# The merge gates and the late projections of a decoder trunk, computed in pairs of column blocks with seven block products in place of eight

## The chip, the cores and the metric

One NeuronCore of a Trainium2 chip runs the kernel. The metric is the device time of one execution in microseconds (us). Before the change it is 2110.89 us, the median of three runs (2110.68 to 2111.18). Engines are called as the profile calls them: PE (TensorE, matmuls), PEld (its weight loads), DVE (VectorE), ACT (ScalarE), POOL (GpSimd) and SP (SyncE, which issues the DMAs).

## The reference, cut

A two-layer decoder trunk on 1024 tokens of width 1024, float32. Each layer runs three token mixers on one normalised input and merges them through gates:

```
h = rms_norm(x, g_pre)
p = h @ w_in                      # 1024 -> 7936 columns
u_a, v_a, gate_a, q_b, k_b, v_b, gate_b, q_c, k_c, v_c, gate_c, merge_logits = split(p)
y_a = chunk_gmlp(u_a, v_a, ...) * silu(gate_a)            # branch A
y_b = sliding_window_attention(rope(q_b), rope(k_b), v_b, sinks) * silu(gate_b)
y_c = stick_breaking_attention(q_c, k_c, v_c) * silu(gate_c)
gates = sigmoid(merge_logits + b_merge)                   # 3 x 1024 columns
merged = gates[0]*(y_a @ w_a) + gates[1]*(y_b @ w_b) + gates[2]*(y_c @ w_c)
x = x + rms_norm(merged @ w_out, g_post)
```

## The kernel before, in words

**Arithmetic.** Every operand of a large matmul is held as two fp32r tiles, a rounded part (hi) and the rest (lo), made by `split` (L101): ACT casts (L104), DVE subtracts (L105). `mm3` (L119 to 123) adds hi x hi, hi x lo and lo x hi into one PSUM bank. So one 128x128 by 128x512 block product is three matmuls of 512 columns, each with its own weight load.

**Layout.** `h`, the normalised input, lies transposed in SBUF for the whole layer: two halves of 512 tokens, each as hi and lo, eight K blocks of 128 in each. One column block of a projection is 128 columns of `w_in`: 2 halves x 8 K blocks x 3 = 48 matmuls of 512 columns. Other data live in 27 slots of 128x1024 (`new`, `done`), reused in the order in which they are given back. PSUM has two banks each under the tags `pj` and `ta` (`ptr`, `pav`), and two tiles of two banks under `z` (`pz`).

**Order.** PE's order is that of the code, fixed by hand. A scheduler orders the other engines. `queue_layer` (L234 to 353) puts projection jobs into a stream, and the branches call `fill(us)` to run so much of that stream between their own steps; `need(label)` runs it until a job is through. All loads and stores are issued by SP in one order.

**Stages of one layer.** Branch C (stick-breaking attention), then branch B (L454 to 572: 8 steps of scores, softmax, two transpositions with POOL selects at L509 and L511, and `attend`, L527), then branch A (L574 to 623, its matmuls at L611 and evacuations at L614), with fills between all steps. Then `merges` (from L638): 24 blocks of 128 output columns, for each half of the tokens 24 gate matmuls from `h` (into `pj`), the sigmoid (L674), 12 branch matmuls (into `pz`), the product of both on DVE (L678, L681) and the sum over branches on POOL (L682). Last `project_out`. `gated` (L625 to 635) multiplies a branch output with its SiLU gate (L630, L631, L632) and splits it.

## Time and profile before

| what | value |
|---|---|
| median of three runs | 2110.89 us |
| the profiled execution, its own time | 2110.61 us |
| its span in the profile | 2108.5 us |
| busy: PE / DVE / ACT / POOL | 2087.3 / 925.2 / 717.1 / 358.6 us |
| matmuls on PE | 10601 |
| moved by DMA | 169.48 MB, mean 80 GB/s |
| layer 1: branch B, branch A, merges | 368 to 536, 536 to 568, 568 to 968 us |
| layer 2: branch B, branch A, merges | 1412 to 1579, to 1612, to 2012 us |

The span is the profiled execution from its first to its last recorded instruction; 2.1 us of its own time lie outside. Busy times are sums over the span, which hold stages of different kinds: what bounds a stage is read from windows, waits and the timeline of that stage. A matmul's recorded duration (0.40 us) is longer than the distance from one start to the next, since matmuls are pipelined.

### The profile page before, as it was taken

To read this page: it belongs to the slowest core of one execution; us is meant where nothing else is said; L and a number is where in the kernel's file an instruction comes from. 1 tells how busy PE (TensorE), PEld (TensorE's weight loads), DVE (VectorE), ACT (ScalarE), POOL (GpSimd) and SP (SyncE) were. 2 spreads that over 40 slices of the span, in tenths; PEclk is the share of its full clock that TensorE was granted. 3 is DMA by queue.
4 is the path that set the end of the run, shared out by engine and by line. 5 is a ranking of instruction groups with operands and counts; after the bars stand their busy time and mean duration, and the time that the engine had idled before them with its cause. 6 is when DMAs were issued, how large, how long until landed. Compare 5 with 4: busy or idle time off the path is not lost.

```text
span 2108.5 us, 25832 instructions
## 1 busy us (share of the span) xinstructions
PE 2087.3 (99%) x10601; PEld 1752.3 (83%) x10601; DVE 925.2 (44%) x1167; ACT 717.1 (34%) x1307; POOL 358.6 (17%) x429
## 2 busy tenths in 40 slices
PE   8999999999999999999999999999999999999998
PEld 7898888898888888888888988888988888888886
DVE  5455543576522423224545545336764233232223
ACT  5334333564322212223334334245552122222221
POOL 0121211443200011110002112105431001111100
PEclk9999999999999999999999999999999999999999
DMA  4112123232412311114321112322234223121123
GB/s 160 41 51 67 54 90 90 70 91 80 170 50 77 114 60 60 40 51 140 109 71 51 41 60 66 95 80 80 71 104 166 60 60 110 50 70 51 47 84 130
DMA packets 162134, 169.48 MB, mean 80 GB/s; under 512 B 5800, under 2 KB 137952, under 8 KB 162016
## 3 DMA queue, kind: packets, MB, share of 16 engines
q1 hardware_dynamic: 162016, 167.83, 25.1%
q8 instruction: 83, 1.36, 0.3%
q14 instruction: 35, 0.29, 0.0%
HBM read 129.01 MB, written 33.55 MB: 77 GB/s over the span
## 4 chain that ended last, share of the span: by engine, by line
PE 97%; DVE 1%; ACT 0%; POOL 0%; DMA 0%; issue 0%; SPq 0%; DVEq 0%; POOLq 0%; ACTq 0%
PE pj L122 24%; PE pj L123 24%; PE pj L121 24%; PE pz L122 5%; PE pz L121 5%; PE pz L123 5%; PE ptr L398 1%; PE pav L527 1%; PE pz L469 1%; PE pav L123 1%; PE pav L122 1%; PE pav L121 1%; PE pz L229 1%; PE ptr L502 1%; DMA s<-in_x_dram 0%; POOL s L511 0%
## 5 line engine op out<-in xcount | busy, mean ns | idle before, releaser
L121 PE MATMUL pj<-h,whi 128*128 128x512 f32 x1728 | 692.4, 401 | 0.0
L122 PE MATMUL pj<-h,whi 128*128 128x512 f32 x1728 | 683.5, 396 | 0.0
L123 PE MATMUL pj<-h,wlo 128*128 128x512 f32 x1728 | 682.6, 395 | 0.0
L123 PEld LDWEIGHTS pj<-h,wlo 128*128 128x128 f32 x1728 | 324.6, 188 | 77.8
L121 PEld LDWEIGHTS pj<-h,whi 128*128 128x128 f32 x1728 | 325.0, 188 | 70.2
L122 PEld LDWEIGHTS pj<-h,whi 128*128 128x128 f32 x1728 | 325.0, 188 | 68.2
L105 DVE TENSOR_TENSOR wlo<-wr,whi 128x1024 fp32r<-128x1024 f32 x148 | 193.4, 1308 | 276.6 <-ACT whi L104 274.3
L104 ACT CAST whi<-wr 128x1024 fp32r<-128x1024 f32 x148 | 154.9, 1050 | 356.3 <-PE pj L122 316.3
L682 POOL TENSOR_TENSOR s<-s,s 128x512 f32<-128x512 f32 x56 | 78.4, 1401 | 659.8 <-DVE s L681 645.5
L121 PE MATMUL pz<-s,whi 128*128 128x512 f32 x384 | 152.0, 396 | 0.0
L122 PE MATMUL pz<-s,whi 128*128 128x512 f32 x384 | 151.7, 395 | 0.0
L123 PE MATMUL pz<-s,wlo 128*128 128x512 f32 x384 | 151.5, 394 | 0.0
L674 ACT ACTIVATE s<-pj,vec 128x512 f32<-128x512 f32 x96 | 65.9, 686 | 240.5 <-PE pj L123 240.5
L121 PE MATMUL pj<-whi,h 128*128 128x256 f32 x512 | 147.1, 287 | 0.0
L123 PE MATMUL pj<-whi,h 128*128 128x256 f32 x512 | 144.1, 281 | 0.6 <-DVE h L105 0.6
L122 PE MATMUL pj<-wlo,h 128*128 128x256 f32 x512 | 144.1, 281 | 0.6 <-DVE wlo L105 0.6
L381 DVE TENSOR_TENSOR_SCAN s<-s,ones 128x128 f32<-128x128 f32 (+3 forms) x64 | 88.4, 1382 | 98.7 <-POOL s L376 98.5
L105 DVE TENSOR_TENSOR s<-ptr,s 128x512 fp32r<-128x512 f32 (+2 forms) x132 | 77.7, 591 | 107.0 <-ACT s L104 106.6
L104 ACT CAST s<-ptr 128x512 fp32r<-128x512 f32 (+2 forms) x132 | 66.8, 506 | 118.0 <-PE ptr L398 110.1
L681 DVE TENSOR_TENSOR s<-s,pz 128x512 f32<-128x512 f32 x64 | 44.0, 687 | 137.8 <-PE pz L123 137.8
L123 PE MATMUL pj<-h,s 128*128 128x512 f32 x256 | 101.6, 397 | 0.0
L121 PE MATMUL pj<-h,s 128*128 128x512 f32 x256 | 101.4, 396 | 0.0
(138 smaller groups left out, 2775.3 us busy)
## 6 DMA issues: line engine op xcount, KB each, us to landing
wr<-in_w_in_dram SPq DMA_DIRECT2D x124, 512.0 KB, 3.8
s<-in_x_dram SPq DMA_DIRECT2D x16, 512.0 KB, 4.9
wor<-in_w_out_dram SPq DMA_DIRECT2D x16, 512.0 KB, 3.7
s<-s SPq DMA_DIRECT2D x40, 128.0 KB, 2.3
gc<-s SPq DMA_DIRECT2D x8, 512.0 KB, 2.7
oc<-s SPq DMA_DIRECT2D x8, 512.0 KB, 3.0
gb<-s SPq DMA_DIRECT2D x8, 512.0 KB, 2.9
ga<-s SPq DMA_DIRECT2D x8, 512.0 KB, 2.7
```

What stands on the lines that cost most here:

```text
L104: nc.scalar.copy(hi, raw)
L105: nc.vector.tensor_tensor(lo, raw, hi.bitcast(F32), op=ALU.subtract)
L121: nc.tensor.matmul(acc, lh, rh, start=first, stop=False)
L122: nc.tensor.matmul(acc, lh, rl, start=False, stop=False)
L123: nc.tensor.matmul(acc, ll, rh, start=False, stop=last)
L229: nc.tensor.transpose(pt[:, k], xn[:, k * P:(k + 1) * P], ident)
L381: nc.vector.tensor_tensor_scan(t1[:, :kl][:, ::-1], t1[:, :kl][:, ::-1], ones.to_broadcast([P, kl]), 1.0, op0=ALU.mult, op1=ALU.mult)
L398: nc.tensor.transpose(pt[:, b - b0], t2[:, b * P:(b + 1) * P], ident)
L469: nc.tensor.matmul(z[:, e * 2 + j], qT[e][:, n * P:(n + 1) * P], kk[i][:, k0:k0 + 256], start=i == 0, stop=i == 1)
L674: nc.scalar.activation(sg[:, ts], a, AF.Sigmoid, bias=bmv(l, xb, dm))
L681: nc.vector.tensor_tensor(sg[:, ts], sg[:, ts], z[:, ts], op=ALU.mult)
L682: eng.tensor_tensor(acc[dm][:, ts], acc[dm][:, ts], sg[:, ts], op=ALU.add)
```

## The change

34 column blocks of `w_in` a layer (two gates of branch B, the four of branch A, the four u blocks of branch A, and all 24 merge gates) leave the stream and the merges. They are computed in one stage, `dense`, behind branch B, in 17 pairs of neighbouring blocks. A pair is a 2x2 block matrix of weights (two K halves by two column blocks) times a 2x2 block matrix of `h` (two K halves by two token halves); Winograd's form of Strassen's method takes seven block products of it and sums ahead of and behind them. `Combine` makes the four sums of `h` blocks (T1 to T4) once a layer, in part during branch B. `prep` makes the seven weight operands of a pair, `prod` is one product of 12 matmuls into a bank of its own, which `bank` takes in turn from three tags (six banks). Branch A is a generator whose steps run between the first products. The SiLU gating of all branches (`gate_task`) runs beside the pairs and stores to DRAM, as do the merge gates after their sigmoid. `merges` keeps only the 12 branch matmuls of each half and loads the gates back. The first half of `w_out` is loaded in the merges (`load_wo`). The fills of branch B are cut to the smaller stream.

```diff
-FB = (10, 1.9, 1.9, 2.5, 3.2, 3.2)
-FB_MORE = {1: 2.3, 2: 1.3}
+FB = (5, 1.5, 1.5, 2.0, 2.6, 2.6)
+FB_MORE = {1: 2.0, 2: 1.0}
...
+    def bank():
+        turn[0] += 1
+        return (pj, ptr, lambda: pz()[:, :512])[turn[0] % 3]()
...
-        hi = wp.tile([P, k, n], F32R, name="whi", tag="whi", bufs=3)
-        lo = wp.tile([P, k, n], F32R, name="wlo", tag="wlo", bufs=3)
+        hi = wp.tile([P, k, n], F32R, name="whi", tag="w", bufs=6)
+        lo = wp.tile([P, k, n], F32R, name="wlo", tag="w", bufs=6)
...
-        gate("b", 0); gate("b", 1); gate("b", 2)
         raw("kb", O_KB, 1.0, after_k)
         raw("vb", O_VB, 1.0, after_v)
-        gate("b", 3)
         for hp in range(4):
             raw(("qb", hp), O_QB + hp * P, 0.125, lambda hp=hp: after_q(hp))
-            if hp < 3:
-                gate("a", hp)
-        va(0); va(1); ua(0); ua(1); ua(2); ua(3); gate("a", 3)
+            if 1 <= hp < 3:
+                gate("b", hp - 1)
+        va(0); va(1)
...
-        need("ga0")
+        need(("qb", 0))
         fill(5)
...
             pend = (v, 1, p1, o)
+            if v >= 4:
+                S["T"].go(3)
         attend(*pend)
...
+    class Combine:
+        def go(self, spare):
+            while self.left and len(free) >= 4 + spare:
+                if next(self.left, "end") == "end":
+                    self.left = None
+        def steps(self):
+            def total(hf, k0, eng):
+                r = new()
+                eng.tensor_tensor(r.rearrange("p (k t) -> p k t", k=2), h[hf][0][:, k0:k0 + 2].bitcast(F32),
+                                  h[hf][1][:, k0:k0 + 2].bitcast(F32), op=ALU.add)
+                return r
...
+            for kp in range(2):
+                k0 = kp * 2
+                r12, r11 = total(1, k0, nc.gpsimd), total(0, k0, nc.gpsimd)
+                nc.vector.tensor_tensor(r11, r12, r11, op=ALU.subtract)
+                keep("T1", r11)
+                yield
+                r22 = total(1, k0 + 4, nc.gpsimd)
+                nc.gpsimd.tensor_tensor(r12, r22, r12, op=ALU.subtract)
+                keep("T3", r12)
...
+                nc.vector.tensor_tensor(r22, r22, r11, op=ALU.subtract)
+                keep("T2", r22)
...
+                r21 = total(0, k0 + 4, nc.gpsimd)
+                nc.vector.tensor_tensor(r21, r21, r22, op=ALU.subtract)
+                keep("T4", r21)
...
+    def dense(l, S):
+        S["T"].go(0)
...
+        def prep(p):
+            col = pairs[p][0]
+            raw = []
+            for q in range(2):
+                t = wp.tile([P, 4, 256], F32, name="wr", tag="wr", bufs=2)
+                nc.sync.dma_start(t, w_in[l, q * 512:(q + 1) * 512, col:col + 256].rearrange("(k p) c -> p k c", p=P))
+                raw.append(t)
+            a11, a21, a12, a22 = (raw[q][:, :, r * P:(r + 1) * P] for q in range(2) for r in range(2))
...
+            yield op(a11)
+            yield op(a12)
...
+            nc.gpsimd.tensor_tensor(s3, a11, a21, op=ALU.subtract)
+            nc.gpsimd.tensor_tensor(a21, a21, a22, op=ALU.add)
+            nc.gpsimd.tensor_tensor(a11, a21, a11, op=ALU.subtract)
+            yield op(a11)
...
+            nc.gpsimd.tensor_tensor(a12, a12, a11, op=ALU.subtract)
+            yield op(a12)
...
+        def prod(n, nm):
+            left(n + 5)
+            w, acc = ops[n], bank()
+            for k in range(4):
+                mm3(acc, (w[:, 0, k], w[:, 1, k]), rhs(nm, k), k == 0, k == 3)
+            return acc
...
+        for p, (col, kind, what) in enumerate(pairs):
...
+            p1 = prod(n, "B11")
+            with tc.high_priority():
+                nc.scalar.copy(c12, p1)
+            add(c11, c12, prod(n + 1, "B21"))
+            add(u2, c12, prod(n + 2, "T2"))
+            if p in then:
+                then[p]()
+            add(u3, u2, prod(n + 3, "T3"))
+            p5 = prod(n + 4, "T1")
+            add(c22, u3, p5)
+            add(u2, u2, p5)
+            add(c21, u3, prod(n + 5, "T4"))
+            add(c12, u2, prod(n + 6, "B22"))
...
+                    nc.scalar.activation(out[j], out[j], AF.Sigmoid, bias=bmv(l, "abc".index(br), dm + j))
+                    nc.sync.dma_start(S["sg"][(i * KD + dm + j) * P:(i * KD + dm + j + 1) * P, :], out[j])
+            done(*out)
+            if p >= 5 and tasks:
+                tasks.popleft()()
+                if p % 2 and tasks:
+                    tasks.popleft()()
...
-                a = pj()
-                for k in range(KD):
-                    mm3(a, (wh[:, k], wlo[:, k]), (h[hf][0][:, k], h[hf][1][:, k]), k == 0, k == KD - 1)
-                nc.scalar.activation(sg[:, ts], a, AF.Sigmoid, bias=bmv(l, xb, dm))
+                z = bank()
                 for c in range(4):
-                    mm3(z[:, ts], (bh[:, c, cs], bl[:, c, cs]), (y[c][0][:, ts], y[c][1][:, ts]), c == 0, c == 3)
+                    mm3(z, (bh[:, c, cs], bl[:, c, cs]), y[c][hf], c == 0, c == 3)
...
             branch_b(l, S)
-            S["yc"] = [gated(S, "c", c) for c in range(4)]
-            branch_a(l, S)
-            while step() is not None:
-                pass
+            dense(l, S)
             mg = merges(l, S)
```

In the rows of instruction order below, `pj`, `ptr`, `pav`, `pz` are PSUM tiles, `h_72` to `h_75` are the four tiles of `h` (first half hi, lo, second half hi, lo), `s_...` are slots, `wr`, `whi`, `wlo` and `wop` are weights (raw, hi, lo, and the seven operands). PE, the end of branch B in layer 1. Before, from the transposes of the last step's first half to the job matmuls behind the last attend:

```order
L502 MATMUL ptr<-ident,s_4560 128x128 x4
L121 MATMUL pj<-h_74,whi 128x512
...
L527 MATMUL pav<-s_4770,s_2932 128x256 x2
L527 MATMUL pav<-s_4771,s_2931 128x256 x2
L527 MATMUL pav<-s_4770,s_2932 128x256 x2
L527 MATMUL pav<-s_4771,s_2932 128x256 x2
L121 MATMUL pj<-h_74,whi 128x512
...
L527 MATMUL pav<-s_4797,s_2932 128x256 x2
L527 MATMUL pav<-s_4798,s_2932 128x256 x2
L527 MATMUL pav<-s_4797,s_2932 128x256 x2
L527 MATMUL pav<-s_4798,s_2932 128x256 x2
L121 MATMUL pj<-h_72,whi 128x512
```

After, from the end of the stream's last job to the first product of `dense`:

```order
L130 MATMUL pj<-whi,h_75 128x256
L500 MATMUL ptr<-ident,s_4000 128x128 x8
L525 MATMUL pav<-s_4292,s_2657 128x256 x4
...
L500 MATMUL ptr<-ident,s_4209 128x128 x8
...
L525 MATMUL pav<-s_4352,s_2658 128x256 x2
L525 MATMUL pav<-s_4364,s_2658 128x256 x2
...
L525 MATMUL pav<-s_4365,s_2658 128x256 x2
L128 MATMUL ptr<-h_72,wop 128x512
L129 MATMUL ptr<-h_73,wop 128x512
```

The gate and projection matmuls of 512 columns that stood between the last transposes, the attends (L527 before, L525 after) and branch A are gone; transposes and attends follow each other, and the first product (`wop`) stands right behind the last attend. From the last scores (not shown) to that product PE has 21 projection matmuls of 256 columns, 38 attend matmuls and 16 transposes.

POOL at the same place. Before, the last selects and the first products of branch A:

```order
L509 AFFINE_SELECT s_4798<-s_4797 128x512
L511 AFFINE_SELECT s_4797<-s_4797 128x512
L509 AFFINE_SELECT s_4798<-s_4797 128x512
L511 AFFINE_SELECT s_4797<-s_4797 128x512
L617 TENSOR_TENSOR s_4550<-s_4550,s_5037 128x512 x2
```

After, from the sums ahead of the selects of step 6 to the first of the last sums for `Combine` (L648 is `total`, L663 the subtraction for T3, L507 and L509 are the selects, L723 to L733 the sums of weights in `prep`):

```order
L648 TENSOR_TENSOR s_4434<-h_72,h_73 128x1024
L648 TENSOR_TENSOR s_4325<-h_74,h_75 128x1024
L663 TENSOR_TENSOR s_3991<-s_4325,s_3991 128x1024
L507 AFFINE_SELECT s_4293<-s_4292 128x512
...
L723 TENSOR_TENSOR s_4451<-wr 128x512
L509 AFFINE_SELECT s_4305<-s_4305 128x512
L507 AFFINE_SELECT s_4306<-s_4305 128x512
L725 TENSOR_TENSOR wr<-wr 128x4x128
...
L648 TENSOR_TENSOR s_4406<-h_72,h_73 128x1024
L509 AFFINE_SELECT s_4364<-s_4364 128x512
...
L509 AFFINE_SELECT s_4364<-s_4364 128x512
L648 TENSOR_TENSOR s_4413<-h_74,h_75 128x1024
```

Sums of whole tiles of `h` and sums of weights now stand among the selects and ahead of the last ones. From the first of these rows to the last select there are 24 instructions: 16 selects, 4 sums of 128x1024 and 4 of 128x512. The last two totals and the last T3 stand behind them.

DVE in one pair of the new stage (L766 is the sum behind a product, L112 the subtraction of `split`, L682 and L684 the two products of `gate_task`):

```order
L766 TENSOR_TENSOR s_5834<-s_5834,ptr 128x512
L112 TENSOR_TENSOR wop<-wr,wop 128x512
L766 TENSOR_TENSOR s_5833<-s_5834,pz 128x512
L112 TENSOR_TENSOR wop<-wr,wop 128x512
L766 TENSOR_TENSOR s_5833<-s_5833,pj 128x512
L112 TENSOR_TENSOR wop<-wr,wop 128x512
L682 TENSOR_TENSOR s_5977<-s_5977,s_5978 128x1024
L766 TENSOR_TENSOR s_5835<-s_5833,ptr 128x512
L766 TENSOR_TENSOR s_5833<-s_5833,ptr 128x512
L112 TENSOR_TENSOR wop<-s_5909,wop 128x512
L684 TENSOR_TENSOR s_5977<-s_5977,s_5978 128x1024
L766 TENSOR_TENSOR s_5835<-s_5833,pz 128x512
```

Before, in the merges of the same layer (L678 the product of gate and branch, L105 the subtraction of `split`):

```order
L678 TENSOR_TENSOR s_5241<-s_5239,pz 128x512
L105 TENSOR_TENSOR wlo<-wr,whi 128x1024
L678 TENSOR_TENSOR s_5241<-s_5239,pz 128x512
L105 TENSOR_TENSOR wlo<-wr,whi 128x1024
L678 TENSOR_TENSOR s_5328<-s_5326,pz 128x512
```

Where DVE had one product per half block and one split of a whole weight tile per block, it now has a split of 128x512 and a sum for nearly every product, with the gating products between them.

## Rows read from the trace of the kernel before

**Rows 1.** The page: busy time of PE and its instructions, and the chain that ended last by engine.

```profile
PE 2087.3 (99%) x10601; PEld 1752.3 (83%) x10601; DVE 925.2 (44%) x1167; ACT 717.1 (34%) x1307; POOL 358.6 (17%) x429
...
PE 97%; DVE 1%; ACT 0%; POOL 0%; DMA 0%; issue 0%; SPq 0%; DVEq 0%; POOLq 0%; ACTq 0%
```

**Rows 2.** All waits of PE over 1 us in the whole span: line that waited, what released it, us in total, times, longest.

```profile
PE pz L229 <- DVE s L220: 9.3, 2, 8.4
PE pav L611 <- DVE s L614: 2.1, 2, 1.0
PE pav L527 <- POOL s L511: 1.8, 2, 0.9
```

**Rows 3.** Windows of layer 1: second half of branch B, branch A, merges. Columns: stretch and length, busy time of PE, PEld, DVE, ACT, POOL with instructions, granted clock, DMA share, GB/s.

```profile
460.00:545.00 85.00, 84.69 (x536) 75.69 (x535) 59.05 (x97) 45.96 (x110) 25.77 (x34) 1.00 0.33 106
545.00:568.00 23.00, 21.96 (x129) 18.88 (x128) 12.03 (x14) 4.11 (x5) 8.76 (x8) 1.00 0.39 129
568.00:968.00 400.00, 400.00 (x1716) 321.94 (x1715) 125.50 (x127) 96.35 (x117) 40.58 (x30) 1.00 0.23 73
```

**Rows 4.** PE's timeline in the merges (first two rows) and in branch B: start, duration, instruction. The 24 matmuls of one gate stand between the first two.

```profile
700.09 0.40 PE L121 MATMUL pj<-h,whi 128*128 128x512 f32 x1
...
705.69 0.39 PE L121 MATMUL pz<-s,whi 128*128 128x512 f32 x1
...
441.65 2.06 PE L469 MATMUL pz<-s,s 128*128 128x256 f32 x16
443.55 0.28 PE L121 MATMUL pj<-whi,h 128*128 128x256 f32 x1
...
448.70 0.60 PE L502 MATMUL ptr<-ident,s 128*128 128x128 f32 x4
449.06 0.36 PE L121 MATMUL pj<-whi,h 128*128 128x256 f32 x1
```

**Rows 5.** Groups of equal instructions over the whole span: line, engine, operation, shapes, count, busy time and mean ns of one, idle time before them and what ended it.

```profile
L105 DVE TENSOR_TENSOR wlo<-wr,whi 128x1024 fp32r<-128x1024 f32 x148 | 193.4, 1308 | 276.6 <-ACT whi L104 274.3
...
L682 POOL TENSOR_TENSOR s<-s,s 128x512 f32<-128x512 f32 x56 | 78.4, 1401 | 659.8 <-DVE s L681 645.5 <-issue 14.3
...
L511 POOL TENSOR_SCALAR_AFFINE_SELECT s<-s 128x512 fp32r<-128x512 f32 x64 | 58.6, 919 | 19.2 <-DVE s L105 11.4 <-issue 3.6 <-POOL s L509 1.9
L105 DVE TENSOR_TENSOR s<-ptr,s 128x512 fp32r<-128x512 f32 x84 | 57.6, 688 | 55.7 <-ACT s L104 55.4
...
L509 POOL TENSOR_SCALAR_AFFINE_SELECT s<-s 128x512 fp32r<-128x512 f32 x64 | 49.9, 782 | 117.8 <-ACT s L104 117.6
...
L681 DVE TENSOR_TENSOR s<-s,pz 128x512 f32<-128x512 f32 x64 | 44.0, 687 | 137.8 <-PE pz L123 137.8
...
L630 DVE TENSOR_TENSOR s<-s,s 128x1024 f32<-128x1024 f32 x24 | 29.8, 1246 | 64.7 <-DMA s<-gb 19.4 <-DMA s<-oa 19.2 <-DMA s<-ga 19.1
...
L282 POOL TENSOR_TENSOR s<-s,s 128x1024 f32<-128x1024 f32 x10 | 25.5, 2545 | 137.1 <-DMA s<-s 107.5 <-PE pj L123 29.6
L104 ACT CAST s<-s 128x1024 fp32r<-128x1024 f32 x24 | 25.2, 1051 | 20.5 <-DVE s L632 17.7 <-POOL s L682 2.7
...
L283 POOL TENSOR_TENSOR s<-s,s 128x1024 f32<-128x1024 f32 x10 | 24.0, 2403 | 0.0
...
L617 POOL TENSOR_TENSOR s<-s,s 128x512 f32<-128x512 f32 x16 | 20.1, 1286 | 51.3 <-DVE s L614 51.3
L104 ACT CAST s<-s 128x512 fp32r<-128x512 f32 x32 | 19.9, 620 | 95.4 <-POOL s L682 88.1 <-DVE s L682 7.3
```

**Rows 6.** A load of weights, from the page's list of DMA issues (KB each, median us to landing), and the window of the highest traffic, at the start (columns as in rows 3).

```profile
wr<-in_w_in_dram SPq DMA_DIRECT2D x124, 512.0 KB, 3.8
...
12.80:15.00 2.20, 2.20 (x11) 1.92 (x10) 1.94 (x2) 2.20 (x5) 0.00 (x0) 1.00 1.02 408
```

**Rows 7.** Timeline near the end of branch B in layer 1, DVE and POOL.

```profile
511.63 0.64 POOL L509 TENSOR_SCALAR_AFFINE_SELECT s<-s 128x512 fp32r<-128x512 f32 x1
...
512.63 1.50 DVE L494 TENSOR_TENSOR s<-s,ls 128x1024 f32<-128x1024 f32 x1
...
513.00 1.62 POOL L509 TENSOR_SCALAR_AFFINE_SELECT s<-s 128x512 fp32r<-128x512 f32 x1
...
514.05 1.65 DVE L105 TENSOR_TENSOR wlo<-wr,whi 128x1024 fp32r<-128x1024 f32 x1
...
514.69 1.50 POOL L511 TENSOR_SCALAR_AFFINE_SELECT s<-s 128x512 fp32r<-128x512 f32 x1
```

**Rows 8.** Timeline of the first rope of the queries in layer 1: ACT empties the bank, SP issues four transfers, POOL and DVE follow.

```profile
351.34 0.59 ACT L268 ACTIVATE s<-pj 128x512 f32<-128x512 f32 x1
...
351.95 2.42 SPq L281 DMA_DIRECT2D s<-s  x4
...
356.29 2.39 POOL L282 TENSOR_TENSOR s<-s,s 128x1024 f32<-128x1024 f32 x1 [29.59 <-PE pj L123]
...
364.81 2.47 DVE L326 TENSOR_TENSOR s<-s,s 64x1024 fp32r<-64x1024 f32 x2
```

**Rows 9.** The last window of the span (columns as in rows 3) and PE's first projection matmuls.

```profile
2106.00:2108.50 2.50, 0.00 (x0) 0.00 (x0) 0.00 (x0) 0.00 (x0) 0.00 (x0) 0.64 0.35 146
...
17.24 0.41 PE L121 MATMUL pj<-whi,h 128*128 128x256 f32 x1
17.45 0.41 PE L122 MATMUL pj<-wlo,h 128*128 128x256 f32 x1
```

More of the change, by code (lines that the diff above doesn't have):

```diff
@@ L602, in branch_a @@
         done(ws)
+        yield
         for g in range(4):
-            need(f"ua{g}")
-            fill(3)
             u, t = S["ua", g], new()
             for hf in range(2):
-                av = (ptr() if hf else pav()).rearrange("p (n t) -> p n t", n=4)
+                av = bank().rearrange("p (n t) -> p n t", n=4)
                 for j in range(4):
@@ new lines, in load_y @@
+    def load_y(S, br, first=False, c=None):
+        y = []
+        if first:
+            S["two"] = [[new(F32R) for _ in range(2)] for _ in range(2)]
+            two = [[t.rearrange("p (c t) -> p c t", c=2) for t in q] for q in S["two"]]
+        for c in range(4) if c is None else [c]:
+            r = new()
+            nc.sync.dma_start(r, S["y" + br][c * P:(c + 1) * P, :])
+            if first:
+                o = [(h[1][0][:, c], h[1][1][:, c]), (two[0][c // 2][:, c % 2], two[1][c // 2][:, c % 2])]
+                for hf in range(2):
+                    split(*o[hf], r[:, hf * HT:(hf + 1) * HT])
+            else:
+                if br == "a":
+                    hi, lo = (t[:, 2 * c:2 * c + 2] for t in h[1])
+                    split(hi, lo, r.rearrange("p (a t) -> p a t", a=2))
+                    o = [(hi[:, hf], lo[:, hf]) for hf in range(2)]
+                else:
+                    hi, lo = new(F32R), new(F32R)
+                    split(hi, lo, r)
+                    S["yslots"].extend((hi, lo))
+                    o = [(hi[:, hf * HT:(hf + 1) * HT], lo[:, hf * HT:(hf + 1) * HT]) for hf in range(2)]
+            done(r)
+            y.append(o)
+        return y
@@ L648, in load, with load_sg @@
                 bi, br, dm = blocks[i]
-                xb = "abc".index(br)
-                wi = load_w(w_in[l, :, O_M + xb * D + dm * P:O_M + xb * D + (dm + 1) * P], KD, P)
-                wl[i] = [wi, load_w(wbs[br][l, :, dm * P:(dm + 2) * P], 4, 256) if dm % 2 == 0 else wl[i - 1][1]]
+                wl[i] = load_w(wbs[br][l, :, dm * P:(dm + 2) * P], 4, 256) if dm % 2 == 0 else wl[i - 1]
+        def load_sg(i):
+            if i < len(blocks) and i not in sgs:
+                bi, br, dm = blocks[i]
+                sgs[i] = new()
+                nc.sync.dma_start(sgs[i], S["sg"][(bi * KD + dm) * P:(bi * KD + dm + 1) * P, :])
         load(0)
-        ys = {"c": S["yc"]}
+        load_sg(0)
+        load_sg(1)
+        ys = {"c": S["first"]}
+        S["yslots"] = []
         for i, (bi, br, dm) in enumerate(blocks):
-            (wh, wlo), (bh, bl) = wl.pop(i) if dm % 2 else wl[i]
+            bh, bl = wl.pop(i) if dm % 2 else wl[i]
             y = ys[br]
-            xb = "abc".index(br)
-            if dm == 0 and bi:
-                for c in range(len(y), 4):
-                    y.append(gated(S, br, c))
-            load(i + 1)
+            for j in (1, 2, 3):
+                load(i + j)
+                load_sg(i + j) if j < 3 else None
+            sg = sgs.pop(i)
             cs = slice((dm % 2) * P, (dm % 2 + 1) * P)
-            sg, z = new(), pz()
             if bi == 0:
@@ L688, in merges @@
                 mg.append((hi, lo))
-            elif dm >= KD - 4:
-                nb = order[bi + 1]
-                if len(free) >= 5:
-                    ys.setdefault(nb, []).append(gated(S, nb, len(ys.get(nb, []))))
-            if dm == KD - 1:
-                for t in y:
-                    done(*t)
+            if bi == 0 and dm < 4:
+                ys.setdefault("b", []).extend(load_y(S, "b", c=dm))
+            if bi == 0 and dm == KD - 1:
+                for t in S["two"]:
+                    done(*t)
+            if bi == 1 and dm < 4:
+                ys.setdefault("a", []).extend(load_y(S, "a", c=dm))
+                load_wo(l, 0, dm * 2)
+            if bi == 1 and dm == KD - 1:
+                done(*S["yslots"])
         return mg
@@ L707, in project_out @@
             nc.sync.dma_start(gpre, g_pre[l + 1].partition_broadcast(P))
-        for q in range(2):
-            for k in range(0, KD, 2):
-                raw = wp.tile([P, 2, 512], F32, name="wor", tag="wr", bufs=2)
-                nc.sync.dma_start(raw, w_out[l, k * P:(k + 2) * P, q * 512:(q + 1) * 512]
-                                  .rearrange("(k p) c -> p k c", p=P))
-                split(h[q][0][:, k:k + 2], h[q][1][:, k:k + 2], raw)
+        for k in range(0, KD, 2):
+            load_wo(l, 1, k)
         o0 = [new() for _ in range(4)]
@@ L813, in trunk @@
     for l in range(L):
-        states.append({nm: dr.tile([512, T], F32, name=f"{nm}{l}") for nm in ("ga", "gb", "gc", "oa", "ob", "oc")})
+        states.append({nm: dr.tile([512, T], F32, name=f"{nm}{l}") for nm in ("ga", "gb", "gc", "oa", "ob", "oc",
+                                                                                "ya", "yb", "yc")})
+        states[l]["sg"] = dr.tile([3 * D, T], F32, name=f"sg{l}")
     nc.scalar.preload_act_table_set("sqrt_and_others")
```

116 lines of the change are left out of this document (95 added, 21 removed).

## The prediction, made before the changed kernel ran

> **What bounds the kernel now.** I read the page's busy line and its chain first: TensorE (PE) is busy 2087.3 of 2108.5 us and holds 97% of the chain that ended last [rows 1]. The waits of PE say how little is lost to others: 9.3 us at the norm (L229), 2.1 us in branch A (L611), 1.8 us in branch B's attends (L527), over two layers [rows 2]. The windows of layer 1 agree stage by stage: 84.69 of 85 us busy in the second half of branch B, 21.96 of 23 in branch A, 400.00 of 400 in the merges, where VectorE (DVE) works 125 us and ScalarE (ACT) 96 [rows 3]. So a matmul taken away is worth its pitch, and a stall put in costs its length, as long as PE stays the bound.
>
> **The pitch.** PE's timeline in the merges starts the first of 24 matmuls of 512 columns at 700.09 and the next group at 705.69: 5.60 / 24 = 0.2333 us each. 16 score matmuls of 256 columns take 441.65 to 443.55, and with what follows them at 0.117 us each; four transposes take 0.36 us [rows 4]. The Trainium skill, page "TensorE: Matmul & The Clock Gate", section "Back-to-back issue gap", gives N/2.4 + 2.5 ns as the gap of one matmul at full clock, 215.8 ns for 512 columns, and about 131 ns in a sustained stream. By these the saving below would be estimated at 88.0 or 53.4 us; the trace shows neither, 233.3 ns, and the sum goes by that.
>
> **What goes.** 34 column blocks a layer took 2 halves x 8 x 3 = 48 matmuls each, 1632. Now 17 pairs take 7 products of 4 x 3 = 12 matmuls, 84 each, 1428. The difference is 204 a layer, 408 in all, x 0.2333 = **95.2 us** of PE. The branch products of the merges keep their number.
>
> **What PE needs from others in a pair.** One pair is 84 x 0.2333 = 19.6 us. By the group rows [rows 5] DVE has 7 splits and 7 adds of 0.69 and, for one and a half branch gates, three products of 1.25: 13.4 us. ACT has 7 casts and a copy of 0.62 (5.0) and some 3.5 activations of a whole tile at 1.05 (3.7): 8.7. GpSimd (POOL) has four 128x512 sums of 1.40: 5.6. Traffic is two 512 KB weight loads, two gate stores and, for one and a half branch gates, at most 2.25 MB, 4.25 MB in 19.6 us = 217 GB/s, where the start of the kernel moved 408, and a weight load lands in 3.8 us [rows 6]. Weight operands are made five products (14 us) ahead and six PSUM banks rotate (the diff). I cost the pair loop at nothing: the cover is PE's own 19.6 us; gone, it costs whatever a pair takes beyond them, 34 times. Merge blocks shrink to 24 x 0.2333 = 5.6 us each with at most 4.7 us of DVE (1.31/2 + 2 x 0.69 + 2 x 1.31) and 2.8 of POOL; also nothing.
>
> **What comes: the tail of branch B.** Before, gate jobs stood between its last transposes and attends. The new order of PE shows none: from the last scores on there are 21 projection matmuls of 256 columns (2.45 us), 38 attend matmuls (4.4) and 16 transposes (1.44), 8.3 us of own work, and then the first product. Meanwhile POOL's new order has, between the sums that wait for the last scores' slots and the last select, 24 instructions: 16 selects at a mean of 0.85 (0.78 and 0.92), 4 sums of 128x1024 at 2.47 and 4 of 128x512 at 1.40 [rows 5]: 13.6 + 9.9 + 5.6 = 29.1 us. The last attend (0.93) follows. PE's stall is 29.1 + 0.9 - 8.3 = **21.7 us a layer**. Lower bound: selects at 0.63 as POOL does them alone [rows 7], sums at 2.40 and 1.29, 24.9 in place of 29.1, so 17.5. Upper bound: rows 7 show a DVE two-input operation at 512.63 taking 1.50 with POOL's select beside it at 1.62, and 1.65 beside 1.50 at 514.05, in place of 0.64 for a select alone: one waits for the other. If all 8.1 us of such DVE work in this stretch stood in POOL's way on top of the 24.9, the stall would be 25.6. I take the means, since they already mix both conditions. The Trainium skill, page "SBUF — State Buffer", section "Who interferes with whom", states that a DVE operation with two SBUF inputs and a GpSimd operation that reads SBUF hold one port pair in turn, for the whole instruction. The trace agrees in rows 7; by that rule the stall would be the upper bound.
>
> **The third product waits for its operand.** It needs T2 of the second half, whose sums POOL makes only behind the last select: 2 x 2.45, DVE 1.31, POOL 2.45, ACT 1.05, and three DVE operations of 1.31, 13.6 us in series [rows 5]. PE covers 0.9 of last attend, two products and 7 matmuls (31 x 0.2333 = 7.2): **5.5 us** wait. With POOL's and DVE's fastest rows it is 5.0; with three weight splits of 0.69 put ahead on DVE it is 7.6.
>
> **Three smaller ones a layer.** Branch B now starts behind the first rope and not behind later jobs: from 351.34, when ACT empties the bank, four transfers of 2.42, POOL 2.39 + 2.40 and DVE up to 367.28 took 16 us [rows 8]; the projections of the next block and the first fill cover most, so 1.0 (0 to 2). In mid-branch the sums for T1 stand on POOL (2 x 2.45) and hold DVE's subtraction ahead of the attends' adds: 2.0 (0 to 4). After a gap the clock can be low: the granted clock is 0.64 in the last stretch, where PE has been idle, and in the first matmuls a 256-column one took 0.21 and not 0.12 [rows 9]; two gaps of such length could cost a few matmuls at half speed: 2.0 (0 to 3). Branch A loses its own stall (21.96 of 23 busy): -1.0.
>
> **The sum.** Per layer 21.7 + 5.5 + 1.0 + 2.0 + 2.0 - 1.0 = 31.2; two layers 62.4. The profiled execution took 2110.61, of which 2108.5 is span and 2.1 lies outside. 2108.5 - 95.2 + 62.4 + 2.1 = 2077.8, and the median of the three runs stands 0.3 above the profiled one: **2078 us**. With all lower bounds a layer costs 21.5 (17.5 + 5.0 - 1.0), 2059; with all upper ones 41.2, 2098. What is late next: POOL's 29 us in the tail makes the sums for the second half late, and that is counted above; the first branch A step, the weights of pair 2 and the loads on SP's queue have 14 us of operands before them.
>
> **Rivals.** *The tail is hidden.* If the scheduler's order lets POOL run sums before the last scores, or PE's 256-column work stretches over them, the tail costs under 20 us a layer, and at nothing the time is 2110.9 - 95.2 = 2015.7. For it: POOL is busy only 25.77 of 85 us in the second half of branch B now [rows 3]. Against it: the sums stand behind the last scores because their slots come free there, and the selects are in POOL's order behind them. *The pair loop does not keep PE's pace*: slower than before. Place: the pair loop, where a weight load is queued on SP behind a gate store that waits for its sigmoid, or a POOL sum and DVE's splits take turns (POOL's 5.6 plus DVE's work with two operands in SBUF, 7 x 0.69 + 3 x 1.25 = 8.6, is 14.2 us of 19.6 in series already). Price: the late time times 34 pairs. From the 2078 there are 33 us left, so it ends even at 0.97 us a pair, and slower beyond 1.1. A product of 2.8 us late once a pair would make 2078 + 95 = 2173. For it: seven operations a product chain over POOL, ACT and DVE; a store waits in the same queue as the loads. Against it: five products of lead, and DVE at 13.4 of 19.6 us. I give the queue 12% and the turns 8%. The rule of the page on SBUF above speaks for the turns, and in rows 7 the trace agrees. *The saving isn't one*: if the seven products' accumulation groups of 12 left a gap at each change of bank, 238 in all, 0.4 us each would give back all of the 95. Against it: 24-matmul groups follow each other now with no gap (705.69 follows at the pitch) [rows 4]; I fold it into the slow case.
>
> **How the numbers follow.** Tail and third product stall as worked out: 62%, 2059 to 2098. Hidden tail: 18%, 2016 to 2059. Pair loop off PE's pace: 20%, 2098 to some 2200. The range leaves out the lower half of the hidden case and the upper half of the slow one, 2 in 10: 2046 to 2110. A measurement tells 0.2%, 4.2 us, from no change. Faster than 2106.7: the first two cases and a quarter of the slow one, 0.85; within 4.2 us 0.05; slower 0.10.
>
> **What the changed profile should show.** PE's matmul count falls by 408 and the merges' stage of branch products lasts some 135 us (24 x 5.6). A wait of PE on a POOL select (the attend's line) of about 20 us, and one on a DVE operation behind the T2 sums of 5 to 6 us, once per layer. In the pairs PE's windows read over 98% busy, a pair in about 19.6 us. Wrong would be: PE waits spread over the weight operands (the loop's own pace), a pitch other than 0.2333 in products of 12, a tail under 10 us, or waits in the merges for gate loads.

## The result: 2119.5 us, slower by 0.4%

The changed kernel takes 2119.51 us (median of seven runs, 2114.68 to 2123.66), the kernel before 2110.68 beside it (seven runs). The ratio is 1.0042, 95% interval 1.003 to 1.0054. The forecast was 2078, with 2046 to 2110 as its range: the saving of 95 us was given back whole and 9 us more. The profiled execution took 2120.2 us, its span is 2117.7.

The page of the kernel after, its busy line, PE's granted clock in 40 slices, and the chain by engine (before: [rows 1]):

```profile
PE 2026.5 (96%) x10193; PEld 1697.3 (80%) x10193; DVE 1239.6 (59%) x1599; ACT 786.1 (37%) x1453; POOL 611.0 (29%) x585
...
PEclk9999999978999999999999999999799999999999
...
PE 87%; DVE 5%; POOL 3%; issue 2%; ACT 1%; DMA 0%; SPq 0%; DVEq 0%; POOLq 0%; ACTq 0%
```

PE has 408 instructions fewer, as the diff says, but 87% of the chain and not 97, and in two places of the span its clock is low. The waits of PE after (line, releaser, total us, times, longest; before: [rows 2]):

```profile
PE pav L525 <- POOL s L509: 26.2, 14, 3.8
PE ptr L500 <- DVE s L536: 14.4, 6, 3.9
PE ptr L500 <- DVE s L112: 9.9, 4, 3.5
PE pj L128 <- ACT s L111: 9.7, 3, 4.3
PE pz L236 <- DVE s L227: 9.3, 2, 8.3
PE ptr L128 <- ACT s L111: 4.2, 1, 4.2
PE ptr L396 <- DVE s L112: 4.0, 2, 2.0
```

L525 and L500 are branch B's attends and transposes, L396 branch C's transposes; of the L128 rows, those released by the cast of a slot (`s L111`) are the T2 product and the first matmuls of `project_out`. Of these rows, two were there before: that of L236, and with 1.8 us that of the attends (L527 there). Windows of layer 1 after: branch C, branch B to its last scores, its tail to the first product, the first 40 us of the pairs, the rest of the pairs and most of the merges, and the way into `project_out` (columns as in rows 3):

```profile
60.00:320.00 260.00, 258.01 (x1429) 221.24 (x1428) 139.68 (x160) 105.17 (x182) 58.92 (x96) 0.99 0.19 58
320.00:448.00 128.00, 120.93 (x812) 111.18 (x811) 89.88 (x131) 65.97 (x195) 64.67 (x61) 0.97 0.18 54
448.00:482.00 34.00, 15.95 (x78) 13.09 (x78) 25.31 (x35) 15.98 (x40) 30.14 (x24) 0.60 0.12 39
482.00:522.00 40.00, 33.91 (x131) 26.74 (x131) 28.34 (x34) 11.19 (x17) 15.33 (x9) 0.87 0.25 86
522.00:946.00 424.00, 424.00 (x1853) 342.78 (x1852) 259.87 (x324) 139.52 (x193) 128.17 (x90) 1.00 0.54 186
946.00:1008.00 62.00, 58.37 (x243) 46.34 (x242) 27.81 (x38) 17.79 (x30) 7.78 (x7) 0.97 0.27 85
```

The same stages before, branch C, branch B to its last scores, and its tail with branch A:

```profile
60.00:368.00 308.00, 308.00 (x1650) 261.83 (x1649) 146.78 (x170) 113.18 (x191) 58.26 (x96) 1.00 0.22 67
368.00:501.00 133.00, 131.80 (x883) 120.11 (x882) 89.34 (x139) 72.92 (x203) 56.77 (x58) 1.00 0.24 72
501.00:568.00 67.00, 65.96 (x347) 55.44 (x346) 39.94 (x54) 28.02 (x54) 22.45 (x25) 1.00 0.42 139
```

The pair loop is at PE's pace: 424.00 of 424 us busy at full clock, with DVE at 260 and POOL at 128. All that was lost lies ahead of it and at its end.

To compare with the forecast's terms I count a stage's loss as the time between its first and last matmul start less its matmuls at full pitch (0.2333, 0.1167, 0.09 for a transpose). The loss holds idle time and matmuls stretched by a low clock alike: in the tail PE stands idle for 34.00 - 15.95 = 18.05 us, and the rest of 25.6 is its own work at the lower clock. The last column sums the gaps over 0.6 us between one start and the next, each less the pitch. Per layer, layer 1 of after:

| term | forecast | measured | of which gaps over 0.6 us |
|---|---|---|---|
| tail of branch B | 21.7 | 25.6 | 21.4, clock 0.60 |
| wait for T2, and the clock behind it | 5.5 + 2.0 | 10.5 | 6.5, clock 0.87 |
| start and middle of B, less branch A's old stall | 1.0 + 2.0 - 1.0 | 12.4 less 6.4 before = 6.0 | 7.0 |
| branch C | 0 | 6.9 less 3.1 before = 3.8 | 2.1 |
| merges into `project_out` | 0 | 5.7 | 3.9 |
| rest of pairs and merges | 0 | 1.2 | 0 |
| sum | 31.2 | 52.8 | |

Layer 2 gives 51.9 in the same way, and 2108.5 - 95.2 + 52.8 + 51.9 = 2118.0 against the span of 2117.7. The account closes, and the saving itself was right.

### The profile page after: what moved, and what is told of

Read it like the earlier page. It is cut to its first block, busy times and chain, and to the rows that moved or that the text cites. A ratio compares the mean times of both kernels' runs of the same rounds, so it can differ in the third digit from the quotient of the medians.

```text
span 2117.7 us, 26645 instructions
## 1 busy us (share of the span) xinstructions
PE 2026.5 (96%) x10193; PEld 1697.3 (80%) x10193; DVE 1239.6 (59%) x1599; ACT 786.1 (37%) x1453; POOL 611.0 (29%) x585
## 4 chain that ended last, share of the span: by engine, by line
PE 87%; DVE 5%; POOL 3%; issue 2%; ACT 1%; DMA 0%; SPq 0%; DVEq 0%; POOLq 0%; ACTq 0%
PE pj L130 16%; PE pj L129 16%; PE pj L128 16%; PE pz L130 6%; PE pz L128 6%; PE pz L129 6%; PE ptr L129 5%; PE ptr L130 5%; PE ptr L128 5%; PE ptr L396 1%; PE pz L467 1%; PE pav L525 1%; PE pav L130 1%; PE pav L129 1%; PE pav L128 1%
## 5 line engine op out<-in xcount | busy, mean ns | idle before, releaser
L128 PE MATMUL pj<-h,whi 128*128 128x512 f32 x700 | 285.8, 408 | 0.0
L112 DVE TENSOR_TENSOR wop<-wr,wop 128x512 fp32r<-128x512 f32 x204 | 187.1, 920 | 158.6 <-ACT wop L111 158.1
L129 PE MATMUL pj<-h,whi 128*128 128x512 f32 x700 | 277.7, 397 | 0.0
L130 PE MATMUL pj<-h,wlo 128*128 128x512 f32 x700 | 277.0, 396 | 0.0
L111 ACT CAST wop<-wr 128x512 fp32r<-128x512 f32 x204 | 125.5, 618 | 310.8 <-DMA wr<-in_w_in_dram 152.2
L130 PEld LDWEIGHTS pj<-h,wlo 128*128 128x128 f32 x700 | 132.0, 189 | 31.5
L128 PEld LDWEIGHTS pj<-h,whi 128*128 128x128 f32 x700 | 132.4, 189 | 24.7
L129 PEld LDWEIGHTS pj<-h,whi 128*128 128x128 f32 x700 | 132.4, 189 | 23.2
L128 PE MATMUL pj<-whi,h 128*128 128x256 f32 x512 | 148.6, 290 | 0.0
L111 ACT CAST whi<-wr 128x1024 fp32r<-128x1024 f32 x80 | 84.0, 1050 | 155.0 <-PE pj L129 80.3
L112 DVE TENSOR_TENSOR wlo<-wr,whi 128x1024 fp32r<-128x1024 f32 x80 | 106.6, 1333 | 54.3 <-ACT whi L111 54.0
L112 DVE TENSOR_TENSOR s<-ptr,s 128x512 fp32r<-128x512 f32 (+2 forms) x132 | 77.8, 591 | 91.0 <-ACT s L111 89.9
L723 POOL TENSOR_TENSOR s<-wr 128x512 f32<-128x512 f32 x34 | 45.4, 1335 | 283.3 <-DMA wr<-in_w_in_dram 209.3
L111 ACT CAST s<-ptr 128x512 fp32r<-128x512 f32 (+2 forms) x132 | 66.9, 507 | 122.2 <-PE ptr L396 112.4
L128 PE MATMUL pj<-h,s 128*128 128x512 f32 x256 | 102.9, 402 | 5.5 <-ACT s L111 5.5
L130 PE MATMUL pj<-h,s 128*128 128x512 f32 x256 | 102.5, 400 | 1.8 <-DVE s L112 1.8
L129 PE MATMUL pj<-h,s 128*128 128x512 f32 x256 | 102.4, 400 | 0.0
```

What stands on the lines that cost most here:

```text
L111: nc.scalar.copy(hi, raw)
L112: nc.vector.tensor_tensor(lo, raw, hi.bitcast(F32), op=ALU.subtract)
L128: nc.tensor.matmul(acc, lh, rh, start=first, stop=False)
L129: nc.tensor.matmul(acc, lh, rl, start=False, stop=False)
L130: nc.tensor.matmul(acc, ll, rh, start=False, stop=last)
L723: nc.gpsimd.tensor_tensor(s3, a11, a21, op=ALU.subtract)
```

## The experiments

**One: cover given back (e1_cover).** The four gates of branch A are jobs of the stream again and branch B's fills have their old sizes.

```diff
-FB = (5, 1.5, 1.5, 2.0, 2.6, 2.6)
-FB_MORE = {1: 2.0, 2: 1.0}
+FB = (10, 1.9, 1.9, 2.5, 3.2, 3.2)
+FB_MORE = {1: 2.3, 2: 1.3}
...
-        va(0); va(1)
+        va(0); va(1); gate("a", 0); gate("a", 1); gate("a", 2); gate("a", 3)
...
-        pairs = [(O_GB + 2 * P, "g", ("b", 2)), (O_UA, "u", 0), (O_UA + 2 * P, "u", 2), (O_GA, "g", ("a", 0)),
-                 (O_GA + 2 * P, "g", ("a", 2))]
+        pairs = [(O_GB + 2 * P, "g", ("b", 2)), (O_UA, "u", 0), (O_UA + 2 * P, "u", 2)]
```

> The four gates of branch A go back into the stream as jobs (15 pairs in place of 17) and the fills of branch B get their old sizes. This gives branch B some 41 us of matmuls a layer to put between its steps, and costs 2 pairs x 12 matmuls x 0.2333 x 2 layers = 11.2 us. Theory 1 (the loss is lost cover: the tail's 25.6 us of waits a layer and the gaps in mid-branch stand bare because the gate jobs are gone): the tail's waits fall under 3 us and the time to 2119.5 + 11 - 2 x (23 + 5) = about 2075, lower still (2055) if the wait for T2 goes too. Theory 2 (POOL's queue is too long whatever PE does): the waits come back later in the branch, the time stays above 2105.

Measured: 2087.59 us (2084.17 to 2090.44), 0.9891 of before (0.9877 to 0.9906). Windows of layer 1, branch B to the last scores, tail, first 40 us of the pairs, and the late pairs with the first merges:

```profile
320.00:455.00 135.00, 131.28 (x878) 119.55 (x878) 94.88 (x147) 69.28 (x198) 65.26 (x61) 1.00 0.22 63
455.00:495.00 40.00, 38.39 (x193) 31.77 (x192) 21.40 (x29) 15.93 (x39) 24.53 (x22) 1.00 0.17 66
495.00:535.00 40.00, 28.84 (x116) 22.52 (x115) 30.22 (x32) 13.58 (x22) 20.41 (x11) 0.87 0.33 109
790.00:930.00 140.00, 137.13 (x584) 108.70 (x583) 80.12 (x96) 40.25 (x47) 35.55 (x25) 1.00 0.62 216
```

The tail's loss falls from 25.6 to 2.2 us with POOL at 24.53 of 40 us, and the middle's from 12.4 to 5.7. That is theory 1. But the time stays 13 us above the expected 2075, for two reasons. The pairs and merges (here 535 to 930 us), where the changed kernel lost 1.3 us a layer, lose 6.2 and 6.0 in the two layers, 2.9 of it idle time in the last window above. And the wait for T2 grew, from 10.5 us with its clock to 13.3 and 13.7: the last row of the timeline below is that product, PE idle for 9.83 us ahead of it. POOL makes weight sums (L722, three more like it) and the two last totals of 128x1024 (L648, 5.78) behind them, and the product's turn comes after 18 matmuls of leftover jobs only.

```profile
493.54 1.30 POOL L722 TENSOR_TENSOR s<-wr 128x512 f32<-128x512 f32 x1 [1.39 <-issue]
...
499.77 5.78 POOL L648 TENSOR_TENSOR s<-h,h 128x1024 f32<-128x1024 f32 x2
...
512.26 0.80 PE L128 MATMUL pj<-s,wop 128*128 128x512 f32 x1 [9.83 <-ACT s L111]
```

**Two: Combine's sums on DVE (e2_sums_dve).**

```diff
-                r12, r11 = total(1, k0, nc.gpsimd), total(0, k0, nc.gpsimd)
+                r12, r11 = total(1, k0, nc.vector), total(0, k0, nc.vector)
```

and the other totals and T3 alike.

> The sums and differences of Combine that POOL makes (10 of 128x1024 a layer) go to DVE, at 1.22 us in place of 2.4; everything else is as in the changed kernel. Theory 2 (POOL's queue and the lock between POOL and DVE set the stalls of branch B): the tail loses four sums of POOL, 9.9 us of 25.6, and the gaps in mid-branch (2.9 to 4.1 us, behind DVE operations that ran 2.3 to 3.3 us beside a POOL sum) vanish: 2119.5 - 2 x (10 + 7 + 3 of clock) = about 2080. Theory 1 (missing cover alone): the chain of softmax, selects and attends is the same, under 5 us a layer are won, 2110 to 2118.

Measured: 2102.61 us (2100.86 to 2105.38), 0.9965 of before (0.9952 to 0.9978). Between the two theories. The middle of branch B lost 6.7 in place of 12.4, as theory 2 had it; the wait for T2 with its clock 8.0 and 8.6 in place of 10.5. The tail hardly moved: 25.4 and 23.7 us in the two layers. Its window shows POOL at 19.25 us and no longer 30, but PE has a new wait there, 7.5 us once a layer, on the softmax's last step on DVE (L492):

```profile
443.00:477.00 34.00, 15.01 (x80) 12.78 (x78) 26.80 (x41) 15.99 (x41) 19.25 (x20) 0.65 0.10 32
```

```profile
PE ptr L500 <- DVE s L492: 15.1, 2, 7.5
```

DVE makes the sums between those steps now; that this makes the wait is not shown. What the sums cost the tail wherever they stand is read from run three, which has none.

**Three: the same stage with eight plain products (e6_plain).** No Combine, no weight sums, no sums behind the products; staging, banks and stream as in the change. `prod` makes 12 matmuls for each half of the tokens.

```diff
-            p1 = prod(n, "B11")
...
-            add(c12, u2, prod(n + 6, "B22"))
+            for r in range(2):
+                accs = [bank(), bank()]
+                for q in range(2):
+                    prod(4 * p + 2 * r + q, q)
                 with tc.high_priority():
...
+                    nc.scalar.copy(out[r][:, :512], accs[0])
+                    nc.vector.tensor_copy(out[r][:, 512:], accs[1])
```

> The same stage and order, but each pair is computed by its eight plain block products: no Combine, no sums of weights on POOL, no sums behind the products. PE gets the 408 matmuls back, 95.2 us. Theory 2 (Combine and prep on POOL make the tail): POOL has 16 selects and nothing else between the last scores and the last attend, 13.6 us at most against 8.3 of PE, the tail's wait falls from 25.6 to 6 or less, the wait for T2 (9 us with its clock) is gone, and the time is 2119.5 + 95.2 - 2 x (20 + 10 + 5) = about 2145. Theory 1 (missing cover alone): the tail keeps 15 us or more, the time is 2165 or more.

Measured: 2176.04 us (2174.45 to 2177.28), 1.0311 of before (1.0295 to 1.0326). Beside the changed kernel with the 95.2 us put back (2214.7) it is 38.7 lower, 19 a layer: what Combine, the weight sums and their splits cost. But it does as much matmul work as the kernel before and is 65 us slower than that, 33 a layer, which the new staging alone costs. Its tail:

```profile
442.00:472.00 30.00, 15.22 (x83) 13.14 (x82) 22.43 (x41) 16.05 (x40) 13.85 (x17) 0.66 0.43 140
```

POOL works 13.85 us of 30, and PE still loses 20.9 (20.5 in layer 2): theory 1, in the tail and in the time. So some 21 of the tail's 25.6 stand without any sum, from scores over exponentials, transposes, splits and selects to the attends of the last two steps, with nothing put between them; taking Combine, the weight sums and their splits away wins only 5.

**Four: the last branch's sums on DVE (e3_last_dve).**

```diff
-                    eng = nc.vector if bi == 2 and dm > KD - 3 else nc.gpsimd
+                    eng = nc.vector if bi == 2 else nc.gpsimd
```

> In the last branch of the merges all sums run on DVE (in the changed kernel POOL makes all but those of the last two blocks). Theory: there a half block's POOL sum 1.29, ACT cast 0.62, DVE split 0.69 and DVE product 0.68 follow each other at 3.4 us a half, while PE now takes 2.8, so project_out finds its last input late: 3.9 us of waits and 1.7 us of low clock a layer, which go: 2119.5 - 11 = 2108. Rival: the wait at the start of project_out is the length of the last block's own chain and stays; the time stays within 3 us of 2119.5.

Measured: 2106.8 us (2105.28 to 2108.52), 12.7 below the changed kernel. The reading behind it is POOL's sum of the last branch in the timeline of the changed kernel, and the larger of the two waits at the start of `project_out`:

```profile
954.95 1.29 POOL L888 TENSOR_TENSOR s<-s,s 128x512 f32<-128x512 f32 x1 [2.11 <-issue]
...
956.27 0.62 ACT L111 CAST s<-s 128x512 fp32r<-128x512 f32 x1 [2.78 <-POOL s L888]
...
956.93 0.69 DVE L112 TENSOR_TENSOR s<-s,s 128x512 fp32r<-128x512 f32 x1 [2.11 <-ACT s L111]
...
957.54 0.68 DVE L885 TENSOR_TENSOR s<-s,ptr 128x512 f32<-128x512 f32 x1
...
958.36 1.29 POOL L888 TENSOR_TENSOR s<-s,s 128x512 f32<-128x512 f32 x1 [2.12 <-DVE s L885]
...
975.38 0.50 PE L128 MATMUL pj<-h,s 128*128 128x512 f32 x1 [2.73 <-ACT s L111]
```

Each link waits for the one above it, DVE's next product (L885) queues behind the split (L112) that waits for ACT, and one round takes 958.36 - 954.95 = 3.41 us. PE needs 2.8 for a half block. Without it the window into `project_out` is full, at full clock:

```profile
946.00:1008.00 62.00, 62.00 (x267) 49.89 (x266) 29.82 (x39) 17.42 (x30) 0.00 (x0) 1.00 0.26 78
```

**Five: matmuls without a use, where PE waits (e5_dummy).** They go to banks that nobody reads.

```diff
+        def idle(n):
+            acc = pj()
+            for _ in range(n):
+                nc.tensor.matmul(acc[:, :256], h[0][0][:, 0, :P], h[0][0][:, 0, :256], start=True, stop=True)
```

> The changed kernel with matmuls that nobody needs put where PE waits: 138 of 256 columns in the tail of branch B (16.1 us a layer at full clock, 25.6 us of waits stood there) and 36 (4.2 us) ahead of the T2 product (6.5 us of waits). PE has 40.6 us more to do in all. Theory (the half clock in the tail and behind it, granted 0.50 for some 31 us and for 6.8 us more a layer, comes from PE's idleness, and costs time of its own): the granted clock stays at or near 1.00 there, the waits for POOL and DVE stay as long, and the time falls by 2 to 6 us a layer, to 2107 to 2116. Rival (the low clock costs nothing, since POOL and DVE set the pace there, or it is not from idleness): the time stays at 2119 or rises, by up to 40.

Measured: 2124.91 us (2123.36 to 2127.38), 1.0069 of before (1.0054 to 1.0084). Tail and first 40 us of the pairs:

```profile
445.00:483.00 38.00, 29.06 (x217) 27.33 (x216) 30.17 (x42) 16.08 (x40) 28.13 (x24) 0.96 0.08 29
483.00:523.00 40.00, 36.15 (x169) 29.47 (x168) 24.28 (x30) 12.04 (x19) 17.33 (x10) 0.96 0.29 92
```

The granted clock is 0.96 in both where it was 0.60 and 0.87: with matmuls in PE's pauses the half clock there is gone. But the tail became 3.8 us longer. That some of the useless matmuls stood ahead of a transpose or attend that was ready, and cost more than the clock gave back, is likely and not shown. How much of the tail the low clock costs is not settled by this run.

**Six and seven: the old order of the gates (e7_best and e8_best_dve).** All gates of branches A and B as jobs, two of them ahead of branch B's projections as in the kernel before, 14 pairs, the gating tasks from pair 4 on, the last branch's sums on DVE; and the same with Combine's sums on DVE.

```diff
+        gate("b", 0); gate("b", 1)
         raw("kb", O_KB, 1.0, after_k)
...
+            if hp < 3:
+                gate("a", hp)
+        va(0); va(1); gate("b", 2); gate("b", 3); gate("a", 3)
```

> All gates of branches A and B are stream jobs again, two of them ahead of branch B's projections as in the kernel before, with the old fills; 14 pairs (4 u blocks, 24 merge gates) in place of 17; the last branch's sums in the merges on DVE. Beside the run with 15 pairs (2087.6): one pair less costs 2.8 a layer, 5.6; project_out's wait goes, -5.7 to -6.9 a layer; and some 43 projection matmuls (10 us) stand between the last attend and the first product, so that the wait for T2 (11.9 us with 1.5 of clock a layer) falls to 0 to 3. Theory (each of these is lost cover): 2087.6 + 5.6 - 12.6 - 2 x 11 = about 2059. Rival (the last sums of Combine start later as well, since they queue behind POOL's selects and weight sums): the T2 wait stays over 8, about 2078.

> As e7_best with Combine's sums on DVE. Theory 1 (with cover restored POOL's sums no longer stand bare): within 6 us of e7_best. Theory 2 (the lock between POOL's sums and DVE still costs in mid-branch): lower by 2 x 3 to 2 x 6 us.

Measured: 2101.96 us (2099.92 to 2103.74) and 2096.32 us (2091.73 to 2096.85). The sixth is far above either expectation, for a reason that neither named; the seventh is 5.6 us lower, on the border of its two theories, and so tells neither from the other. The T2 wait is gone, with 42 matmuls in front of it, and so is the wait at `project_out`; the loss is now in branch B, 8.6 us a layer just ahead of its first scores and 19 from there to its last ones. Waits of PE in the sixth run:

```profile
PE pz L468 <- DVE s L333: 28.3, 8, 7.7
PE ptr L501 <- DVE s L537: 10.3, 4, 4.3
```

L333 is the last operation of the rope of the queries. The change starts branch B when the first query projection is through, `need(("qb", 0))`, where the kernel before waited for the gate job behind it. With two gates put ahead of the projections, the first query is through later (ACT empties its second bank at 328.14 us, in the changed kernel at 305.74, well inside branch C), and only the 5 us of `fill(5)` stand between it and its scores. The rope, 1.0 a layer in the forecast, costs 28.3 / 2 = 14 us a layer of waits in this order. Branch C, on the other hand, is back at the loss it had before the change: it has no wait in either run.

**Eight and nine: cover, in the order of the change (e9_cover14 and e10_cover15).** 14 pairs, branch B's gates 2 and 3 as the last jobs (114 matmuls left behind the last attend, all but the last job's ahead of the first weight operands), the gating tasks from pair 4 on; and 15 pairs with fills a tenth smaller (42 left). In both, Combine's and the last branch's sums on DVE.

```diff
+        va(0); va(1); gate("a", 0); gate("a", 1); gate("a", 2); gate("a", 3); gate("b", 2); gate("b", 3)
```

> The run with 15 pairs (2087.6) with the gates 2 and 3 of branch B as jobs behind the others (14 pairs), Combine's sums on DVE and the last branch's sums of the merges on DVE; the order of jobs is otherwise that of the 15 pairs, without the earlier gates that put the rope's chain ahead of the scores in e7_best. 115 matmuls (27 us) stand between the last attend and the first product. Theory (cover): +5.6 for the pair, -12.6 for project_out, -2 x 13 for the T2 wait, 0 to -6 for the sums: 2050 to 2056. Rival (branch B's start again waits for the rope, as in e7_best, 17 us a layer): 2080 or more.

> 15 pairs, Combine's sums and the last branch's sums on DVE, fills of branch B a tenth smaller than before, so that 43 matmuls (10 us) are left behind the last attend for the T2 chain of about 11 us with DVE's sums. Theory (cover): 2087.6 - 12.6 - 2 x 11 - 0 to 6 + 2 for smaller fills: 2049 to 2055. Rival (fills a tenth smaller bring the gaps of branch B back): the waits in branch B grow from 5.7 to 9 or more a layer, 2062.

Measured: 2047.23 us (2046.47 to 2050.02), 0.9703 of before (0.9688 to 0.9717), and 2048.76 us (2047.61 to 2051.99), 0.9709 (0.9693 to 0.9725). Both just below the lower end of what was expected. The eighth in layer 1, branch B to the last scores, tail with leftover jobs, first 40 us of pairs:

```profile
320.00:456.00 136.00, 132.83 (x880) 121.18 (x879) 99.09 (x150) 68.94 (x198) 57.38 (x58) 0.99 0.22 63
456.00:517.00 61.00, 61.00 (x291) 50.20 (x290) 45.80 (x52) 25.58 (x52) 24.46 (x21) 1.00 0.27 95
517.00:557.00 40.00, 40.00 (x175) 32.35 (x175) 22.46 (x31) 13.80 (x21) 11.03 (x8) 1.00 0.30 94
```

Tail and T2 wait are at nothing, at full clock. Three pairs fewer cost 3 x 12 x 0.2333 x 2 = 16.8 us of the saving; with the two moves to DVE the kernel is 72 us below the changed one, so cover and moves bring 89. It is 63 us below the kernel before. Run nine, with 15 pairs, lies 1.5 us above it, within the scatter of both, and its T2 wait is gone as well, with 42 matmuls in front. Beside run one it differs by the moves to DVE and the smaller fills alone, and these bring 39 us; which of them brings how much, beyond the 12.7 of run four, was not tried.

## Why the prediction was wrong, step by step

**The saving and the pair loop: right.** 408 matmuls at 0.2333 are gone, and the pairs run at 424.00 of 424 us. The rival of a pair loop off PE's pace did not happen in the changed kernel; the time landed in its range by another way. In run one there are first signs of it: gaps of 1.2 and 1.7 us near the last pairs of layer 1, the first for a weight operand. The rival of a hidden tail did not happen: PE stands idle for 18.05 of 34 us there.

**Where it left the range.** The forecast's own terms came out near their upper bounds together: tail, T2 with its clock and the middle of branch B make 25.6 + 10.5 + 6.0 = 42.1 a layer, where its upper bounds make 41.2. That alone would have given some 2100, inside the range. The step that failed is that the merges were put at nothing, and that branch C, which the new stream also feeds, got no term: these (5.7 and 3.8) and the rest of the pairs (1.2) cost 10.7 a layer, 21 us in all.

**The tail: near in size, and right for this kernel, not as a cause.** "PE's stall is 29.1 + 0.9 - 8.3 = 21.7 us a layer" against 25.6 measured, the stated upper bound. In the changed kernel POOL's queue is what ended last: its 24 instructions take from 448.42 to 480.42 us, 32.0 in place of 29.1. The 16 selects took 1.01 us at the mean and not 0.85, a group for each of the two lines:

```profile
L507 POOL TENSOR_SCALAR_AFFINE_SELECT s<-s 128x512 fp32r<-128x512 f32 x8 | 8.5, 1068 | 0.9 <-ACT s L111 0.9
L509 POOL TENSOR_SCALAR_AFFINE_SELECT s<-s 128x512 fp32r<-128x512 f32 x8 | 7.6, 952 | 0.4
```

But the step made the sums in that queue the cause, and without them it would leave 13.6 + 0.9 - 8.3 = 6.2. Run three measured 20.9: the chain of softmax, splits and selects through ACT, DVE and POOL in turns is nearly as long as the queue. What decides is that no projection work is left for PE. With work left the same stretch costs 2.2 us (run one, POOL's sums in it) and 0.4 (run eight). That the queue and the chain are about equally long, so that the size came out near, was luck.

**T2: right in kind, 5.5 forecast, 6.5 of gaps measured;** with the clock behind it 10.5. Run eight closes it: 114 matmuls in front, and nothing is left; in runs six and nine 42 are enough, in run one 18 are not.

**The clock: too small.** I allowed 2.0 a layer for it. Beyond the tail, half-clock stretches of 3.4 us stood behind the waits in branch C, branch B and `project_out`, where PE is busy. Such a stretch cost 1.6 of its 3.4 us: branch C loses 6.9 us with one and 5.3 in run one, with the same wait and none.

**The middle of branch B: 2.0 net forecast, 6.0 measured.** Two conditions came together, and taking either away is enough: with Combine's sums off POOL (run two) 12.4 falls to 6.7, with the fills back (run one) to 5.7, where the kernel before has 6.4, branch A's stall included. In the changed kernel's timeline a DVE operation of 128x8 stood 2.32 us beside two POOL sums of 2.45 each, and PE waited 2.8 us for the input of the transposes behind it (at 420.26); in the last step of the branch the same operation took 0.17:

```profile
410.22 4.91 POOL L648 TENSOR_TENSOR s<-h,h 128x1024 f32<-128x1024 f32 x2 [4.36 <-PE pz L467]
...
412.83 2.32 DVE L485 SCALAR_TENSOR_TENSOR mx<-mx,nsnk 128x8 f32<-128x8 f32 x1
...
451.03 0.17 DVE L485 SCALAR_TENSOR_TENSOR mx<-mx,nsnk 128x8 f32<-128x8 f32 x1
```

This is the lock that [rows 7] show. The Trainium skill, page "SBUF — State Buffer", section "Who interferes with whom", has the loser blocked for the other's whole instruction; the trace agrees here, 2.32 us beside 2.45, for an operation as small as 128x8. I weighed it for the tail and not for the softmax chain of the whole branch. The fills cut in the diff's first lines I had read as following the smaller stream, and gave them no price.

**Costed at nothing and wrong: the merges, 5.7 a layer, and branch C, 3.8.** "Merge blocks shrink to 24 x 0.2333 = 5.6 us each with at most 4.7 us of DVE ... and 2.8 of POOL; also nothing." Each engine's sum fits; the round through POOL, ACT and DVE in order does not, 3.41 against 2.8. Run four shows it: 12.7 us. In branch C PE waits 2.1 us for a split behind DVE's work on the key rope, which the shorter stream has moved to this place. That wait stands in every run with this stream, and it is gone in both layers of runs six and seven, whose stream has two gates ahead of the key projection again: there branch C loses what it lost before the change. So the order of the stream is the cause; that it acts through the key rope is read from the timeline alone.

Of the 21.6 us a layer that were missing, the two terms at nothing and the rest make 10.7, the middle of B 4.0, the tail 3.9, T2 and its clock 3.0.

## What to carry to other kernels

A job that is moved out of a filler stream is charged twice: what it costs in its new place, and what stood bare where it had been. Price the second from the chain that it covered, as if that were run with nothing between its steps, and keep so many fillers that the last step of the chain, and the first thing that waits behind it, are covered: here two pairs of 17 given back, with the old fills, turned 9 us lost into 23 won, and two or three, with sums moved from POOL to DVE, into 62 and 63. When a stage gets shorter on the bounding engine, compare its new pace with the longest round through the others in order, not with each one's sum.
